# Differential attention with three 128-column products in one PSUM sum, and one reciprocal per attention job

## The chip, the cores and the metric

The kernel runs on one core of one Trainium2 chip. The metric is the device time of one execution in microseconds (us); the median of three runs is used. The core has five engines with an instruction queue each: TensorE (PE, with its weight loads shown apart as PEld), VectorE (DVE), ScalarE (ACT), GpSimd (POOL) and SyncE (SP), which here only issues transfers between the main memory and the on-chip memory. Each queue runs in the order in which it was written; engines wait for each other by semaphores.

## The reference

One layer on x of 1024 tokens by 1024 features: half of a SwiGLU feed-forward block is added, then a mixer, then half of a second feed-forward block, then a norm. The mixer is two attentions side by side. The part that matters:

```
# A: 8 heads of 64, each token sees its chunk of 64 and the 8 chunks before
p = softmax(q k^T / 8 + bias);  o = p v
# B: 4 heads; each has two score sets (q, k of 64) and values v of 128
p = softmax(scores_r + bias)                    # r = 0, 1
attn = p[0] - lam * p[1];  o = attn v
o = rms_norm(o, subln_g) * (1 - lambda_init)
# both
merged = sigmoid(g_A) * (o_A W_A) + sigmoid(g_B) * (o_B W_B)
x = x + merged W_o
```

## The kernel before, in words

All matrix products work on float32 values that are split in two parts, `hi` (rounded) and `lo` (what is left), and a product a·b is formed as hi·hi + hi·lo + lo·hi. The helper `mm3` (L125 to L129) writes these three matmuls into one PSUM sum. The stages follow each other: first feed-forward block, input projection of the mixer, the two attentions, branch and output projections, second feed-forward block, final norm.

The change lies in the attention stage, which runs from about 1121 to 1401 us of the span. Its work is cut in jobs of 128 or 256 query rows. `run` starts a new job at each step and moves up to four live jobs on by one piece each, so scores and softmax of one job stand beside the transposes, value products and norms of older ones. This fixes only the order in which the program is written: the framework then plans each engine's queue with an own model of durations, and so a change in one place reorders all five queues of the stage.

- `jobs_a` makes 32 jobs (8 heads, 4 blocks of 256 rows). A job computes two score tiles `sc`, in `softmax` a minimum on DVE (L692) and the exponential with its row sum `rs` on ACT (L694), then `ri`, the reciprocal of `rs` (L749, DVE), and scales the probabilities `pm` by it on POOL (L750). Two pieces later come the transposes `pt` (L700, PE) with their split in `whi` (ACT) and `wlo` (DVE), and then the value products `pv` (L766).
- `jobs_b` makes 32 jobs (4 heads, 8 blocks of 128 rows; block i sees i + 1 blocks of 128 keys, called kb here, so a head has 36 and the stage 144). It takes two softmaxes, two reciprocals (L824, L826), and forms p[0] + r2·p[1] on DVE (L827, L829), where r2 holds -lam and the ratio of the row sums. After the transposes the values are multiplied. Here `vt` holds the values as 256 columns, first the hi part, then the lo part, and before the change one matmul takes all 256 of them:

```
nc.tensor.matmul(pv, pt[0][:, c], vt[:, kb, :], start=kb == 0, stop=False)                            # L845
nc.tensor.matmul(pv[:, 0:P], pt[1][:, c], vt[:, kb, 0:P], start=False, stop=kb == i)                  # L846
```

  So the left half of `pv` holds hi·hi + lo·hi and the right half hi·lo; two ACT copies (L848, L850) scale them by r1 and POOL adds them (L851). Then follow a sum of squares (L854, DVE), a power and a product on POOL (L138, L857), the transposing product `try` (L860, PE) and the split into `y`.
- `branch_a` is a filler: the output projection of A (`pb`, twelve matmuls of 512 columns each, then a product with the gate `gl` on DVE, L794, and a store `ta`, L795). Every second job of B draws one of its 16 parts.
- The first job of a head loads q, k (hi and lo) and v in `load_qkv` (L123): `qs`, `ks`, `kl`, `vt`, 1 MB each, the first three as two halves. They lie in a pool of 14 buffers of that size, which also holds the results `y` and the bias `nb`. SP issues the loads in its own order, among the loads `gl` and `wa` and the stores `ta`, which wait for DVE.

The pools `rs` and `ri` have four buffers of a few bytes. Before, a job of B takes two of each; the reciprocal r1 is in use until the copies L848 and L850.

Of the kernel before, what the change touches and what calls it, by code (L numbers as in the profile page):

```python
# [53 lines left out]
def hybrid_layer_kernel(ctx, tc, x, ffn1_norm, ffn1_w_in, ffn1_w_out, mix_norm, w_mix_in,  # L54
# [601 lines left out]
    with tc.tile_pool(name="ps2", bufs=1, space=PSUM) as ps:  # L656
# [31 lines left out]
        def softmax(sc, n, nb, dst, rs):  # L688

            mn = small.tile([P, 1], F32, tag="mn", name="mn")  # L690
            d3 = dst.rearrange("p (n w) -> p n w", n=n)
            nc.vector.tensor_tensor_reduce(out=d3, in0=sc, in1=nb.rearrange("p (n w) -> p n w", n=n),  # L692
                                           scale=1.0, scalar=3e38, op0=ALU.add, op1=ALU.min, accum_out=mn)
            nc.scalar.activation(out=dst, in_=dst, func=AF.Exp, bias=mn, scale=-1.0, accum_out=rs)  # L694
# [26 lines left out]
        def jobs_a(pr):  # L721
            ctx_ = {}

            def job(sb_, h):
                if not ctx_:
                    ctx_["qkv"] = load_qkv(pr)
                    ctx_["y"] = big([P, 2, S], "y")
                    ys.append(ctx_["y"])
                    ctx_["nb"] = big([P, 2, S], "nb", F32)
                    for hh in range(2):  # L730
                        bias_rows(ctx_["nb"][:, hh, :WA], diag_a, 2 * pr + hh, EA, WA)
                qkv, y, nb = (ctx_[n] for n in ("qkv", "y", "nb"))
                vt = qkv[3]
                i0, i1 = 2 * sb_, 2 * sb_ + 1
                first = [max(0, i - 4) for i in (i0, i1)]

                slots = [(kb, s) for kb in range(first[1], i0 + 1) for s in range(2)]
                if first[0] < first[1]:
                    slots.append((first[0], 0))
                slots.append((i1, 1))  # L740
                pms = []
                for s, i in enumerate((i0, i1)):
                    w = (i - first[s] + 1) * P
                    sc, n = scores(qkv, h, i, first[s] * P, w)
                    pm = raw_tile([P, D], "pm")[:, :w]
                    rs = small.tile([P, 1], F32, tag="rs", name="rs")
                    softmax(sc, n, nb[:, h, WA - w:WA], pm, rs)
                    ri = small.tile([P, 1], F32, tag="ri", name="ri")
                    nc.vector.reciprocal(out=ri, in_=rs)  # L749
                    nc.gpsimd.tensor_tensor(out=pm, in0=pm, in1=ri.to_broadcast([P, w]), op=ALU.mult)  # L750
                    pms.append(pm)
                yield
                yield
                pts = []
                for u0 in range(0, len(slots), 4):
                    pts.append(transpose_p([pms[s][:, (kb - first[s]) * P:(kb - first[s] + 1) * P]
                                            for kb, s in slots[u0:u0 + 4]]))
                yield
                pv = ps.tile([P, 256], F32, tag="pv", bufs=2, name="pv")
                b = 0  # L760
                while b < len(slots):
                    kb, s = slots[b]
                    nq = 2 if b + 1 < len(slots) and slots[b + 1][0] == kb else 1
                    o = (b % 4) * P
                    for c in range(2):
                        nc.tensor.matmul(pv[:, s * P:(s + nq) * P], vt[:, kb, 128 * h:128 * h + 128],  # L766
                                         pts[b // 4][c][:, o:o + nq * P], start=(b == 0 and c == 0),
                                         stop=(b + nq == len(slots) and c == 1))
                    b += nq

                if h == 0:
                    ctx_["ysum"] = temp([P, 256], "ysum")
                ysum = ctx_["ysum"]
                rh, rl = slice(64 * h, 64 * h + 64), slice(64 - 64 * h, 128 - 64 * h)
                nc.scalar.copy(out=ysum[rh, :], in_=pv[rl, :])
                nc.vector.tensor_tensor(out=ysum[rh, :], in0=pv[rh, :], in1=ysum[rh, :], op=ALU.add)
                if h == 1:
                    c = slice(sb_ * 256, (sb_ + 1) * 256)
                    split(ysum, y[:, 0, c], y[:, 1, c], on_pool=True)
            return [job(sb_, h) for sb_ in range(4) for h in range(2)]  # L780


# [16 lines left out]
        def jobs_b(hb, filler):  # L799
            ctx_ = {}  # L800

            def job(i):
                if not ctx_:
                    ctx_["qkv"] = load_qkv(4 + hb)
                    ctx_["y"] = big([P, 2, S], "y")
                    ys.append(ctx_["y"])
                    if hb % 2 == 0:
                        nbs.append(big([P, 2, S], "nb", F32))
                        for hh in range(2):
                            bias_rows(nbs[-1][:, hh, :], diag_b, hb + hh, EB, WB)  # L810
                    ctx_["nb"] = nbs[-1][:, hb % 2, :]
                qkv, y, nb = (ctx_[n] for n in ("qkv", "y", "nb"))
                vt = qkv[3]
                w = (i + 1) * P
                pr, rs = [], []
                for r in range(2):
                    sc, n = scores(qkv, r, i, 0, w)
                    pm = raw_tile([P, WB], "pm")[:, :w]
                    s_ = small.tile([P, 1], F32, tag="rs", name="rs")
                    softmax(sc, n, nb[:, WB - w:], pm, s_)  # L820
                    pr.append(pm)
                    rs.append(s_)
                r1, r2 = (small.tile([P, 1], F32, tag="ri", name="ri") for _ in range(2))
                nc.vector.reciprocal(out=r1, in_=rs[0])  # L824

                nc.vector.reciprocal(out=r2, in_=rs[1])  # L826
                nc.vector.scalar_tensor_tensor(out=r2, in0=r2, scalar=neg_lam, in1=rs[0],  # L827
                                               op0=ALU.mult, op1=ALU.mult)
                nc.vector.scalar_tensor_tensor(out=pr[0], in0=pr[1], scalar=r2, in1=pr[0],  # L829
                                               op0=ALU.mult, op1=ALU.add)  # L830
                yield
                yield
                pts = []
                for b0 in range(0, i + 1, 4):
                    pts.append(transpose_p([pr[0][:, b * P:(b + 1) * P] for b in range(b0, min(b0 + 4, i + 1))]))
                due[0] += 0.5
                while due[0] >= 1:
                    due[0] -= 1
                    next(filler, None)
                yield  # L840
                pv = ps.tile([P, 256], F32, tag="pv", bufs=2, name="pv")
                for kb in range(i + 1):
                    c = slice((kb % 4) * P, (kb % 4 + 1) * P)
                    pt = pts[kb // 4]
                    nc.tensor.matmul(pv, pt[0][:, c], vt[:, kb, :], start=kb == 0, stop=False)  # L845
                    nc.tensor.matmul(pv[:, 0:P], pt[1][:, c], vt[:, kb, 0:P], start=False, stop=kb == i)  # L846
                o1 = temp([P, P], "o1")
                nc.scalar.activation(out=o1, in_=pv[:, P:], func=AF.Copy, scale=r1)  # L848
                o2 = temp([P, P], "o2")
                nc.scalar.activation(out=o2, in_=pv[:, :P], func=AF.Copy, scale=r1)  # L850
                nc.gpsimd.tensor_tensor(out=o1, in0=o1, in1=o2, op=ALU.add)  # L851
                sq = temp([P, P], "sq")
                v = small.tile([P, 1], F32, tag="v", name="v")
                nc.vector.tensor_tensor_reduce(out=sq, in0=o1, in1=o1, scale=1.0 / P, scalar=EPS,  # L854
                                               op0=ALU.mult, op1=ALU.add, accum_out=v)
                dg = small.tile([P, P], F32, tag="dg", bufs=3, name="dg")
                nc.gpsimd.tensor_tensor(out=dg, in0=ident, in1=rsqrt(v).to_broadcast([P, P]), op=ALU.mult)  # L857
                yield
                tr = ps.tile([P, 4, P], F32, tag="pt", bufs=2, name="try")
                nc.tensor.matmul(tr[:, 0, :], o1, dg, start=True, stop=True)  # L860
                c = slice(i * P, (i + 1) * P)
                split(tr[:, 0, :], y[:, 0, c], y[:, 1, c], scale=gsub)
            return [job(i) for i in range(NT)]
# [115 lines left out]
```

## Time and profile before

| | |
|---|---|
| median of three runs | 2207.89 us (2207.6 to 2208.07) |
| the profiled execution | 2210.82 us, its span 2209.0 us |
| PE, PEld busy | 95%, 81% of the span |
| DVE, ACT, POOL busy | 66%, 45%, 13% |
| granted TensorE clock, mean | 0.979 |
| main memory | 144 GB/s over the span |

The span is the time from the first to the last instruction of the profiled execution. "Busy" adds the times of instructions; matmuls are pipelined, so that a matmul's own time overlaps the next one's, and the distance between the starts of two neighbours says what one of them costs. In a row of the trace, "[5.34 <-DMA ks<-k]" means that the engine stood idle for 5.34 us just before and what ended that. In the tables of waits the columns are the total in us, the number of waits and the longest. In tables of stretches each engine has its busy time and the number of its instructions in brackets, and behind them stand the granted clock, the share of the 16 transfer engines that is busy, and GB/s.

### The profile page before, as it was taken

The page shows a single profiled execution, that of the slowest core. Times are in us where ns is not written, and L with a number is a line of the kernel's source. Part 1 is how long each engine was busy: PE and PEld are TensorE (multiplying, and loading weights), DVE is VectorE, ACT ScalarE, POOL GpSimd, SP SyncE. Part 2 cuts the span into 40 slices and gives each one's busy share as a digit, 9 for nine tenths or more (in the row PEclk, how much of TensorE's full clock was granted, in tenths as well). Part 3 has the DMA queues.
Part 4 walks back from the last instruction along what each step waited for, and adds up shares of the span by engine and source line. Part 5 has one row for each costly group of instructions (what it writes and reads, how often), then busy time and mean ns, then how long its engine had stood idle before and what let it go on. Part 6 is the DMA issues. An engine that isn't in the chain of part 4 may idle for free. (4 is left out here: it accounts for less than half of the span.)

```text
span 2209.0 us, 29778 instructions
## 1 busy us (share of the span) xinstructions
PE 2100.4 (95%) x10373; PEld 1779.8 (81%) x10373; DVE 1448.2 (66%) x2620; ACT 991.2 (45%) x1972; POOL 286.4 (13%) x371
## 2 busy tenths in 40 slices
PE   5999999999997999999999988899799999999997
PEld 4888888888886998888878877788688888888886
DVE  8765656577567756655378877658756565658566
ACT  5433333334445444444478756335433333334444
POOL 6130000000006100000056333104300000000000
PEclk8999999999998999999999989999999999999999
DMA  4374323284353445542497555755423232367335
GB/s 136 100 198 115 119 83 118 96 305 162 115 154 112 134 154 171 172 148 91 120 226 184 125 152 139 225 166 172 119 86 120 88 116 93 111 224 240 97 115 186
DMA packets 262246, 319.72 MB, mean 145 GB/s; under 512 B 16732, under 2 KB 162156, under 8 KB 262096
## 3 DMA queue, kind: packets, MB, share of 16 engines
q1 hardware_dynamic: 257888, 309.91, 45.3%
q0 software_dynamic: 4064, 7.39, 1.5%
q8 instruction: 82, 1.34, 0.3%
q14 instruction: 68, 0.56, 0.1%
q10 hardware_dynamic: 144, 0.52, 0.1%
HBM read 219.44 MB, written 98.30 MB: 144 GB/s over the span
## 5 line engine op out<-in xcount | busy, mean ns | idle before, releaser
L101 DVE TENSOR_TENSOR wlo<-raw,whi 128x512 fp32r<-128x512 f32 x197 | 141.6, 719 | 183.3 <-PE prod L128 109.7
L96 ACT CAST whi<-raw 128x512 fp32r<-128x512 f32 x200 | 124.4, 622 | 273.8 <-PE prod L128 224.5
L96 ACT CAST whi<-T 128x512 fp32r<-128x512 f32 x192 | 119.5, 623 | 282.7 <-PE prod L128 163.0
L128 PE MATMUL po<-wlo,whi 128*128 128x512 f32 x616 | 240.0, 390 | 0.0
L129 PE MATMUL po<-whi,wlo 128*128 128x512 f32 x616 | 239.9, 390 | 0.0
L127 PE MATMUL po<-whi 128*128 128x512 f32 x616 | 236.4, 390 | 0.0
L101 DVE TENSOR_TENSOR wlo<-T,whi 128x512 fp32r<-128x512 f32 x189 | 134.2, 710 | 98.3 <-ACT whi L96 74.4
L112 DVE TENSOR_TENSOR c<-prod,c 128x512 f32<-128x512 f32 (+1 forms) x201 | 133.2, 664 | 99.7 <-PE prod L129 98.7
L101 DVE TENSOR_TENSOR wlo<-B,whi 128x512 fp32r<-128x512 f32 x154 | 107.0, 695 | 129.2 <-ACT whi L96 129.2
L96 ACT CAST whi<-B 128x512 fp32r<-128x512 f32 x154 | 95.7, 622 | 206.9 <-PE po L128 185.3
L138 POOL TENSOR_TENSOR r<-v,neg_half 128x1 f32<-128x1 f32 x64 | 44.3, 693 | 758.9 <-DVE v L155 721.2
L129 PEld LDWEIGHTS po<-whi,wlo 128*128 128x128 f32 x616 | 115.7, 188 | 24.1
L127 PEld LDWEIGHTS po<-whi 128*128 128x128 f32 x616 | 115.7, 188 | 23.9
L128 PEld LDWEIGHTS po<-wlo,whi 128*128 128x128 f32 x616 | 115.7, 188 | 23.8
L184 POOL TENSOR_TENSOR xt<-xt,gain 128x512 f32<-128x512 f32 x36 | 49.1, 1380 | 516.4 <-DMA xt<-xm 484.3
L96 ACT CAST whi<-ha 128x512 fp32r<-128x512 f32 x154 | 94.8, 616 | 39.0 <-PE prod L128 17.2
L101 DVE TENSOR_TENSOR wlo<-ha,whi 128x512 fp32r<-128x512 f32 x154 | 105.7, 687 | 10.0 <-ACT whi L96 10.0
L258 ACT COPY c<-prod 128x512 f32<-128x512 f32 (+1 forms) x201 | 103.3, 573 | 5.2 <-issue 2.6
L694 ACT ACTIVATE pm<-pm,mn 128x640 f32<-128x640 f32 (+7 forms) x128 | 94.1, 736 | 17.4 <-DVE mn L692 16.1
L127 PE MATMUL prod<-S1h,whi 128*128 128x512 f32 (+1 forms) x252 | 96.5, 383 | 2.2 <-ACT S1h L96 2.2
L127 PE MATMUL prod<-S4h,whi 128*128 128x512 f32 (+1 forms) x252 | 96.1, 381 | 1.8 <-ACT c L258 1.8
L127 PE MATMUL prod<-A11h,whi 128*128 128x512 f32 (+1 forms) x252 | 96.8, 384 | 0.7 <-ACT A11h L96 0.7
(247 smaller groups left out, 5835.4 us busy)
## 6 DMA issues: line engine op xcount, KB each, us to landing
raw<-in_ffn_w_in_dram SPq DMA_DIRECT2D x88, 512.0 KB, 3.9
ha<-hS SPq DMA_DIRECT2D x88, 256.0 KB, 2.7
raw<-in_w_mix_in_dram SPq DMA_DIRECT2D x40, 512.0 KB, 4.1
ha<-hA SPq DMA_DIRECT2D x66, 256.0 KB, 2.7
hA<-c SPq DMA_DIRECT2D x64, 256.0 KB, 2.5
B<-in_ffn_w_out_dram SPq DMA_DIRECT2D x12, 1024.0 KB, 5.9
hS<-hs SPq DMA_DIRECT2D x44, 256.0 KB, 2.1
hS<-c SPq DMA_DIRECT2D x42, 256.0 KB, 2.1
```

Of the source, the lines that this page charges most:

```text
L96: nc.scalar.copy(out=hi, in_=src)
L101: (nc.gpsimd if on_pool else nc.vector).tensor_tensor(out=lo, in0=src, in1=h, op=ALU.subtract)
L112: nc.vector.tensor_tensor(out=out_, in0=a, in1=b, op=op)
L127: nc.tensor.matmul(ps, a[0], b[0], start=first, stop=False, skip_group_check=shared)
L128: nc.tensor.matmul(ps, a[0], b[1], start=False, stop=False, skip_group_check=shared)
L129: nc.tensor.matmul(ps, a[1], b[0], start=False, stop=last, skip_group_check=shared)
L138: nc.gpsimd.tensor_tensor(out=r, in0=v, in1=neg_half, op=ALU.pow)
L184: (nc.vector if on_vector else nc.gpsimd).tensor_tensor(out=xt[h][d], in0=xt[h][d], in1=gain[:, c], op=ALU.mult)
L258: nc.scalar.copy(out=self.held[name], in_=p)
L694: nc.scalar.activation(out=dst, in_=dst, func=AF.Exp, bias=mn, scale=-1.0, accum_out=rs)
```

## The change

In B the two matmuls of a kb become the three of `mm3`, each with 128 columns, all into one `pv` of 128 columns; the second ACT copy and the POOL sum go. In both attentions the row sums of a job's two softmaxes lie in one tile `rs` of two columns, and one reciprocal takes both; in A the two POOL products follow it. Since a job now takes one `rs` and one `ri`, the four buffers hold four jobs of B, where they held two.

```
@@ jobs_a
-                pms = []
+                pms, rs = [], small.tile([P, 2], F32, tag="rs", name="rs")
                 for s, i in enumerate((i0, i1)):
...
-                    rs = small.tile([P, 1], F32, tag="rs", name="rs")
-                    softmax(sc, n, nb[:, h, WA - w:WA], pm, rs)
-                    ri = small.tile([P, 1], F32, tag="ri", name="ri")
-                    nc.vector.reciprocal(out=ri, in_=rs)
-                    nc.gpsimd.tensor_tensor(out=pm, in0=pm, in1=ri.to_broadcast([P, w]), op=ALU.mult)
+                    softmax(sc, n, nb[:, h, WA - w:WA], pm, rs[:, s:s + 1])
                     pms.append(pm)
+                ri = small.tile([P, 2], F32, tag="ri", name="ri")
+                nc.vector.reciprocal(out=ri, in_=rs)
+                for s, pm in enumerate(pms):
+                    nc.gpsimd.tensor_tensor(out=pm, in0=pm, in1=ri[:, s:s + 1].to_broadcast(list(pm.shape)),
+                                            op=ALU.mult)
@@ jobs_b
-                r1, r2 = (small.tile([P, 1], F32, tag="ri", name="ri") for _ in range(2))
-                nc.vector.reciprocal(out=r1, in_=rs[0])
-                nc.vector.reciprocal(out=r2, in_=rs[1])
-                nc.vector.scalar_tensor_tensor(out=r2, in0=r2, scalar=neg_lam, in1=rs[0],
+                ri = small.tile([P, 2], F32, tag="ri", name="ri")
+                r1, r2 = ri[:, 0:1], ri[:, 1:2]
+                nc.vector.reciprocal(out=ri, in_=rs)
+                nc.vector.scalar_tensor_tensor(out=r2, in0=r2, scalar=neg_lam, in1=rs[:, 0:1],
                                                op0=ALU.mult, op1=ALU.mult)
@@ jobs_b, value product
-                pv = ps.tile([P, 256], F32, tag="pv", bufs=2, name="pv")
+                pv = ps.tile([P, P], F32, tag="pv", bufs=2, name="pv")
                 for kb in range(i + 1):
                     c = slice((kb % 4) * P, (kb % 4 + 1) * P)
-                    pt = pts[kb // 4]
-                    nc.tensor.matmul(pv, pt[0][:, c], vt[:, kb, :], start=kb == 0, stop=False)
-                    nc.tensor.matmul(pv[:, 0:P], pt[1][:, c], vt[:, kb, 0:P], start=False, stop=kb == i)
+                    mm3(pv, [v[:, c] for v in pts[kb // 4]], (vt[:, kb, 0:P], vt[:, kb, P:]), kb == 0, kb == i)
                 o1 = temp([P, P], "o1")
-                nc.scalar.activation(out=o1, in_=pv[:, P:], func=AF.Copy, scale=r1)
-                o2 = temp([P, P], "o2")
-                nc.scalar.activation(out=o2, in_=pv[:, :P], func=AF.Copy, scale=r1)
-                nc.gpsimd.tensor_tensor(out=o1, in0=o1, in1=o2, op=ALU.add)
+                nc.scalar.activation(out=o1, in_=pv, func=AF.Copy, scale=r1)
```

The planned order moves in the whole attention stage. Three places matter below. The first is TensorE where the second head of B ends and the third begins: the row with `sc` of 128 columns, twice, is the third head's first score. Before:

```order
L845 MATMUL pv<-vt,whi 128x256
L846 MATMUL pv<-vt,wlo 128x128
L700 MATMUL pt<-ident,pm 128x128
L845 MATMUL pv<-vt,whi 128x256
L684 MATMUL sc<-ks,qs 128x128 x2
L860 MATMUL try<-dg,o_12353 128x128
L846 MATMUL pv<-vt,wlo 128x128
L845 MATMUL pv<-vt,whi 128x256
```

and the same place now, where `pv` comes from the lines of `mm3`:

```order
L128 MATMUL pv<-vt,whi 128x128
L129 MATMUL pv<-vt,wlo 128x128
L127 MATMUL pv<-vt,whi 128x128
L128 MATMUL pv<-vt,whi 128x128
L684 MATMUL sc<-ks,qs 128x128 x2
L700 MATMUL pt<-ident,pm 128x128 x4
L129 MATMUL pv<-vt,wlo 128x128
L685 MATMUL sc<-kl,qs 128x128 x2
L700 MATMUL pt<-ident,pm 128x128 x2
```

The `try` and the value products of one older job that stood behind the new head's first score now stand ahead of it, and the second half of that score (L685, which needs `kl`) follows it closely.

The second place is SP's queue where the fourth head of B is loaded (`q_182`, `k_190`). The `ta` rows are the stores that wait for DVE.

```order
+L796 DMA ta_213<-gl 128x512
+L118 DMA wa<-in_w_branch_a_dram 128x4x256
 L118 DMA gl<-g_197 128x512
-L118 DMA wa<-in_w_branch_a_dram 128x4x256
-L795 DMA ta_213<-gl 128x512
 L123 DMA qs<-q_182 64x2x1024
 L123 DMA ks<-k_190 64x2x1024
 L123 DMA qs<-q_182 64x2x1024
 L123 DMA ks<-k_190 64x2x1024
+L796 DMA ta_213<-gl 128x512
+L118 DMA gl<-g_198 128x512
 L123 DMA kl<-k_190 64x2x1024 x2
```

The second store `ta_213` stood ahead of the four loads and now stands behind them.

The third is DVE in the second job pair of A (the `ISA` rows are the minimum of `softmax` and the reading of its result):

```order
 L692 ISA pm,mn<-sc,nb 128x384
 L692 ISA mn 128x1
-L749 RECIPROCAL ri<-rs 128x1
 L692 ISA pm,mn<-sc,nb 128x512
 L692 ISA mn 128x1
-L749 RECIPROCAL ri<-rs 128x1
+L749 RECIPROCAL ri<-rs 128x2
 L101 TENSOR_TENSOR wlo<-pt,whi 128x384
```

One of the two reciprocals is gone, and the one left stands at the place of the later one.

More of the change, by code (lines that the diff above doesn't have):

```diff
@@ L814, in job @@
                 w = (i + 1) * P
-                pr, rs = [], []
+                pr, rs = [], small.tile([P, 2], F32, tag="rs", name="rs")
                 for r in range(2):
@@ L818, in job @@
                     pm = raw_tile([P, WB], "pm")[:, :w]
-                    s_ = small.tile([P, 1], F32, tag="rs", name="rs")
-                    softmax(sc, n, nb[:, WB - w:], pm, s_)
+                    softmax(sc, n, nb[:, WB - w:], pm, rs[:, r:r + 1])
                     pr.append(pm)
-                    rs.append(s_)
-                r1, r2 = (small.tile([P, 1], F32, tag="ri", name="ri") for _ in range(2))
-                nc.vector.reciprocal(out=r1, in_=rs[0])
-                nc.vector.reciprocal(out=r2, in_=rs[1])
-                nc.vector.scalar_tensor_tensor(out=r2, in0=r2, scalar=neg_lam, in1=rs[0],
+                ri = small.tile([P, 2], F32, tag="ri", name="ri")
+                r1, r2 = ri[:, 0:1], ri[:, 1:2]
+                nc.vector.reciprocal(out=ri, in_=rs)
+                nc.vector.scalar_tensor_tensor(out=r2, in0=r2, scalar=neg_lam, in1=rs[:, 0:1],
                                                op0=ALU.mult, op1=ALU.mult)
```

## The prediction

> **What bounds the kernel now.** I read the page first, then the table of stretches over the attention stage, the waits of TensorE there, and the trace row by row where the table shows a hole.
>
> ```profile
> span 2209.0 us, 29778 instructions
> 1121.00:1234.70 113.70, 104.89 (x737) 92.77 (x736) 98.54 (x308) 96.48 (x250) 71.42 (x89) 0.98 0.74 170
> 1234.70:1254.96 20.26, 18.18 (x109) 15.54 (x107) 18.99 (x52) 15.38 (x39) 7.37 (x14) 1.00 1.02 229
> 1254.96:1298.57 43.61, 36.31 (x219) 32.42 (x219) 32.89 (x105) 24.88 (x66) 13.30 (x23) 0.92 0.66 160
> 1298.57:1347.02 48.45, 40.37 (x224) 35.47 (x224) 33.76 (x107) 27.75 (x74) 13.45 (x26) 0.86 0.61 166
> 1347.02:1397.50 50.48, 46.13 (x293) 40.51 (x293) 41.60 (x127) 31.70 (x86) 19.93 (x34) 1.00 0.45 147
> ```
>
> The first stretch is A, the other four are the heads of B, cut where the next head's `kl` lands. In A nothing is full: PE is busy for 104.9 of 113.7 us with overlap counted in, DVE for 98.5, ACT for 96.5. In B, PE leads DVE in all heads but the first (46.1 against 41.6 us in the last), ACT and POOL have much room. The profiled execution took 2210.82 us, 1.82 more than its span and 2.93 more than the median of 2207.89; I carry differences over to the median.
>
> PE in B has two kinds of holes, those of the loads of the next head and small ones:
>
> ```profile
> PE sc L684 <- DMA ks<-k: 11.1, 2, 5.7
> PE pv L845 <- ACT o L850: 3.0, 6, 0.7
> PE sc L685 <- DMA kl<-k: 1.7, 2, 1.2
> PE pv L845 <- DVE ri L824: 1.4, 1, 1.4
> ```
>
> ```profile
> 1254.96 0.44 PE L685 MATMUL sc<-kl,qs 128*128 128x128 f32 x2 [1.17 <-DMA kl<-k]
> ...
> 1294.88 0.69 PE L684 MATMUL sc<-ks,qs 128*128 128x128 f32 x2 [5.34 <-DMA ks<-k]
> 1298.57 0.63 PE L685 MATMUL sc<-kl,qs 128*128 128x128 f32 x2
> ...
> 1342.40 0.66 PE L684 MATMUL sc<-ks,qs 128*128 128x128 f32 x2 [5.72 <-DMA ks<-k]
> 1347.02 0.41 PE L685 MATMUL sc<-kl,qs 128*128 128x128 f32 x2 [0.54 <-DMA kl<-k]
> ```
>
> So B is PE work in a row, stopped at each new head until its loads land. More PE work lengthens B, except for what fits into those stops.
>
> **The change part by part: the value products.** The cost of one matmul is the distance between starts:
>
> ```profile
> 1392.10 0.33 PE L845 MATMUL pv<-vt,whi 128*128 128x256 f32 x1
> 1392.27 0.22 PE L846 MATMUL pv<-vt,wlo 128*128 128x128 f32 x1
> 1392.33 0.34 PE L845 MATMUL pv<-vt,whi 128*128 128x256 f32 x1
> ```
>
> ```profile
> 1233.40 0.28 PE L766 MATMUL pv<-whi,vt 128*128 128x128 f32 x1
> 1233.51 0.27 PE L766 MATMUL pv<-wlo,vt 128*128 128x128 f32 x1
> ```
>
> ```profile
> L845 PEld LDWEIGHTS pv<-vt,whi x144: 186/189/334, 1234.7 to 1397.0; 128*128 128x128 f32 x144
> L846 PEld LDWEIGHTS pv<-vt,wlo x144: 187/192/338, 1234.8 to 1397.1; 128*128 128x128 f32 x144
> ```
>
> A pair L846, L845 takes 0.23 us (1392.10 to 1392.33), with two weight loads: 0.115 us a load. Two products of 128 columns with a load each (1233.40 to 1233.51) take 0.11 too. Halving the columns thus saves nothing; the load sets the pace, and every matmul has its own, as the 144 and 144 loads show. The change makes three loads of the two: 144 more, 144 x 0.115 = 16.6 us more PE work. By the order these fall as 15, 36, 36 and 57 in the four stretches, other PE work staying the same in each: 1.7, 4.1, 4.1 and 6.6 us. The ends of the unknown are nothing, if the third matmul only takes the 0.06 between 1392.27 and 1392.33 and the fuller pipeline hides that, and all 16.6.
>
> The Trainium skill ("TensorE: Matmul & The Clock Gate", Back-to-back issue gap) gives about 81 ns a matmul for a stream of load and matmul pairs with 128 columns. By it three would be 243 ns and the change 144 x 13 ns = 1.9 us, an estimate from that page; the 0.11 us between the rows above speaks against it.
>
> What a stop takes up depends on when the loads start, and SP's queue sets that:
>
> ```profile
> 1245.40 0.62 SPq L123 DMA_DIRECT2D kl<-k  x1
> ...
> 1276.38 0.32 SPq L795 DMA_DIRECT2D ta<-gl  x1
> ...
> 1277.22 0.58 SPq L123 DMA_DIRECT2D qs<-q  x1
> ...
> 1334.12 1.22 SPq L123 DMA_DIRECT2D kl<-k  x2
> ```
>
> First head, +0.6 us. The stop ends with `kl`, issued at 1245.40 and landed at 1254.96. Its issue stays behind the same store, while a transfer of `wa` now goes ahead; 1.7 us of work meet 1.17 us of idle time. Between 0 and 1.7.
>
> Second head, +2.0. The loads of the third head start at 1277.22, when the store of a filler part is through. In the order, DVE's product for that part now stands behind one more score, and PE has 63 value matmuls ahead of that score instead of 42: 21 x 0.115, and four score matmuls at no less than a load each, 0.5, make it 2.9 us later. Against that `wa` now follows the bias instead of preceding `vt`, which frees the transfer engines somewhat; I take 0.9 us for it. PE itself waits 5.34 us here and so takes up its 4.1 us. Between 0 and 4.1.
>
> Third head, +1.0. `qs` and `ks` no longer wait for a second store, so they should be there in time, and `kl` decides: its buffer comes free with the old head's last score, which now has 93 value matmuls ahead of it within the head, not 55, and four more transposes: 42 loads of 0.115 = 4.8 us later. `kl` took 12.9 us from 1334.12 to 1347.02, queued behind `qs` and `ks`; without them the nearest price is the 9.6 us of 1245.40, 3.3 less. That leaves 1.5, less a share of the small waits, 0.5. Between -1.7 (`kl` in half of its 12.9 us) and +4.8.
>
> Last head, +4.0. No load follows, so 6.6 us of work go on the path. Off go waits: `pv` has two buffers, and a new one had to wait for the second copy. The six waits of 3.0 us in all become shorter by the 0.25 us by which the second copy ends after the first (below), half of them here, 0.75; the 1.4 us of L824 goes, since four jobs' reciprocals now have room; 0.4 for better filling. Between +2 and +6.6.
>
> **Copies, sum and reciprocals.**
>
> ```profile
> 1397.46 0.37 ACT L848 ACTIVATE o<-pv,ri 128x128 f32<-128x128 f32 x1 [1.76 <-PE pv L846]
> 1397.72 0.36 ACT L850 ACTIVATE o<-pv,ri 128x128 f32<-128x128 f32 x1
> 1398.16 0.45 POOL L851 TENSOR_TENSOR o<-o,o 128x128 f32<-128x128 f32 x1 [0.50 <-ACT o L850]
> 1398.91 0.28 DVE L854 CUSTOM_DVE_ANT_0 sq<-o 128x128 f32<-128x128 f32 x1
> ```
>
> ```profile
> L850 ACT ACTIVATE o<-pv,ri 128x128 f32<-128x128 f32 x32 | 11.6, 364 | 0.0
> L851 POOL TENSOR_TENSOR o<-o,o 128x128 f32<-128x128 f32 x32 | 15.8, 493 | 78.4 <-ACT o L850 78.4
> L749 DVE RECIPROCAL ri<-rs 128x1 f32<-128x1 f32 x64 | 9.7, 155 | 3.3 <-ACT pm L694 3.0
> ```
>
> The 11.6 us of ACT and 15.8 of POOL lie under PE, which has the longest busy time in three heads of B; they show only in the last job, where nothing covers the chain from copy to norm. There the square starts at 1398.91; without L850 and L851 it starts about 0.3 after the first copy's end at 1397.83, at 1398.1: -0.8 us.
>
> In A, 32 of 64 reciprocals of 0.155 us go: 5.0 us of DVE, which is busy for 87% of A. All 5.0 would come off if DVE alone bounded A, none if the chain through ACT and PE did, and it is near both; I take the middle, -2.5. The first `pm` of a job is now scaled about one softmax later, but the order has two more jobs' scores between reciprocal and transposes, so POOL (71 of 113.7 us) has cover; if that cover were gone, PE would wait in A, at worst about +1. In B 32 reciprocals go, under PE: nothing.
>
> Sum: 0.6 + 2.0 + 1.0 + 4.0 - 0.8 - 2.5 = +4.3 us. From 2210.82 that is 2215.1 for a profiled execution, and 2212.2 against the median, so 2212.
>
> **The rivals.** (1) Nothing is taken up. If the loads of each head start later by as much as PE's work grows, the stops stay as long as they are: +16.6 - 0.8 - 2.5 = +13.3, 2221 us. For it: the stores ahead of the loads wait on filler work that stands behind PE's. Against it: only 2 to 5 us of delay can be counted up to those places.
>
> (2) The stops take up more, and the clock stays up. After the stop in the second head the granted clock is half:
>
> ```profile
> 1296.00:1300.00 4.00, 3.78 (x19) 3.38 (x18) 1.10 (x4) 1.67 (x6) 0.11 (x1) 0.50 1.08 307
> 1300.00:1304.00 4.00, 4.00 (x19) 4.00 (x20) 2.30 (x8) 1.44 (x4) 2.27 (x3) 0.50 1.06 393
> ```
>
> From `kl` at 1298.57 to 1304 it costs 5.4 / 2 = 2.7 us. If the extra work shortens the idle 5.34 us enough, that returns. With A at its best (-5.0), the first two heads at 0, the third at -2.7 and the last at +2: -6.5 with the tail, 2201 us. The point from which it decides is whether PE's idle time at 1289 to 1295 gets short enough to keep the clock; the trace has no stop between 1.2 and 5.3 us that would tell.
>
> The Trainium skill ("TensorE: Matmul & The Clock Gate", What's actually happening) has the clock fall to half after an idle window of about 3.4 us. By that page, 5.34 - 2.1 us of net filling would stay just below it, an estimate.
>
> (3) The third product is nearly free: with the same `whi` as its neighbour it costs no load of its own. Then the heads gain only: -0.8 - 2.5 - 2.2 for the waits, 2202.4 us. Against it: every matmul in the trace has its load, also L127 and L128 of `mm3`, which share theirs. The Trainium skill's 81 ns above belongs here.
>
> **How the numbers follow.** What can be told from no change in this kernel is about 0.2%, 4.4 us. My forecast, chance 0.48, own range 2208 to 2217 by the bounds of its terms taken half each way, lies at the upper edge of that: 0.32 within, 0.16 slower. Rival 1 gets 0.26, slower. Rival 2 gets 0.16: 0.12 faster, 0.04 within. Rival 3 gets 0.10: 0.06 faster, 0.04 within. Together 0.18 faster, 0.40 the same, 0.42 slower. The range 2202 to 2222 reaches from rival 3 to a little past rival 1.
>
> **What would show it.** Right: `pv` in B with 432 matmuls and 432 loads at 0.115 us; the third stop shorter than 5.72 us; the last head longer by about 4; A shorter by about 2.5. Wrong: triples at 0.23 us (rival 3); stops as long as before in all heads and B longer by 16 (rival 1); a clock of 1.00 after the second head's stop (rival 2). It also goes wrong if the new order of A makes PE wait for POOL, or if SP's new order delays a load by more than the few us counted here.

## The result, and the profile after

The changed kernel is slower: 2230.71 us against 2207.98 us (medians of four runs each), a ratio of 1.0096 with a 95% interval of 1.0075 to 1.0117. That is 22.7 us more, where 4 us more were forecast, and above the forecast range. The profiled execution took 2230.97 us, 20.2 more than the profiled one of before.

The table of stretches, cut at the same events as in the prediction (A, then the heads of B at the landing of the next head's `kl`), for the changed kernel; behind the engines' columns stand the granted clock, the share of the transfer engines and GB/s:

```profile
span 2229.2 us, 29929 instructions
1119.50:1233.10 113.60, 105.49 (x742) 92.24 (x741) 97.29 (x278) 97.17 (x252) 71.78 (x89) 1.00 0.75 171
1233.10:1259.00 25.90, 20.16 (x119) 17.39 (x118) 17.61 (x46) 14.16 (x33) 4.53 (x9) 0.93 0.81 189
1259.00:1308.95 49.95, 43.81 (x255) 39.57 (x255) 34.80 (x100) 23.82 (x60) 8.72 (x16) 0.84 0.52 126
1308.95:1358.54 49.59, 42.85 (x258) 39.22 (x259) 33.14 (x98) 25.03 (x65) 9.47 (x18) 0.84 0.67 180
1358.54:1419.40 60.86, 58.28 (x350) 52.20 (x350) 40.10 (x116) 28.64 (x72) 13.01 (x23) 0.87 0.36 115
```

A is as long as before (113.6 against 113.7 us). The heads of B are longer by 5.6, 6.3, 1.1 and 10.4 us. The column of the clock shows what the forecast left out: 0.93, 0.84, 0.84 and 0.87, where before it was 1.00, 0.92, 0.86 and 1.00.

The value products cost what was said. The tile `pv` in the changed kernel (least, median and longest ns of one load, first and last start):

```profile
L127 PEld LDWEIGHTS pv<-vt,whi x144: 186/192/338, 1233.1 to 1419.1; 128*128 128x128 f32 x144
L128 PEld LDWEIGHTS pv<-vt,whi x144: 187/192/333, 1233.2 to 1419.2; 128*128 128x128 f32 x144
L129 PEld LDWEIGHTS pv<-vt,wlo x144: 188/192/338, 1233.3 to 1419.3; 128*128 128x128 f32 x144
```

There are 432 loads, L127 and L128 with the same `whi` among them. TensorE's rows around the three stops of the changed kernel (the places where it waits for a new head's loads) and one small wait near the end show the rest:

```profile
1252.45 0.28 PE L128 MATMUL pv<-vt,whi 128*128 128x128 f32 x1
1255.93 0.69 PE L684 MATMUL sc<-ks,qs 128*128 128x128 f32 x2 [3.19 <-DMA ks<-k]
...
1259.00 0.69 PE L685 MATMUL sc<-kl,qs 128*128 128x128 f32 x2 [0.96 <-DMA kl<-k]
...
1302.86 0.28 PE L128 MATMUL pv<-vt,whi 128*128 128x128 f32 x1
...
1306.53 0.69 PE L684 MATMUL sc<-ks,qs 128*128 128x128 f32 x2 [3.40 <-DMA ks<-k]
...
1351.97 0.45 PE L684 MATMUL sc<-ks,qs 128*128 128x128 f32 x1 [2.52 <-issue]
1355.53 0.47 PE L684 MATMUL sc<-ks,qs 128*128 128x128 f32 x1 [3.11 <-DVE mn L692]
...
1395.80 0.28 PE L128 MATMUL pv<-vt,whi 128*128 128x128 f32 x1
1395.91 0.27 PE L129 MATMUL pv<-vt,wlo 128*128 128x128 f32 x1
...
1398.27 0.33 PE L127 MATMUL pv<-vt,whi 128*128 128x128 f32 x1 [1.28 <-ACT o L845]
...
1399.15 0.41 PE L128 MATMUL pv<-vt,whi 128*128 128x128 f32 x1
1399.36 0.41 PE L129 MATMUL pv<-vt,wlo 128*128 128x128 f32 x1
```

At full clock a value product costs 0.11 us (1395.80 to 1395.91), after the last wait 0.21 (1399.15 to 1399.36). Stretches of the changed kernel at those four places, from the point where the clock has just fallen:

```profile
1255.50:1269.00 13.50, 11.38 (x46) 10.44 (x47) 6.96 (x26) 5.00 (x16) 1.50 (x3) 0.50 0.59 163
...
1303.30:1316.90 13.60, 9.62 (x45) 9.24 (x45) 3.96 (x15) 3.92 (x12) 1.34 (x5) 0.50 1.01 290
...
1351.10:1364.60 13.50, 8.40 (x26) 6.88 (x27) 6.63 (x21) 3.84 (x11) 0.95 (x2) 0.50 0.79 206
...
1398.90:1408.90 10.00, 9.61 (x41) 8.80 (x41) 3.88 (x10) 2.47 (x6) 2.59 (x4) 0.50 0.75 248
```

The second stop became shorter (3.40 us, 5.34 before), the third is as long in two parts (2.52 and 3.11 around one matmul, 5.72 before), and the first, 1.17 us before, grew to 3.19 with 0.96 behind it. With each go 13.5 us or more at half clock, and with the pause of 1.28 us another 10. The clock does not wait for a stop to end: it has fallen by 1255.5, 2.7 us into the first stop, and by 1303.3, when the second had only begun (its last matmul before started at 1302.86 and took 0.28). In the kernel before there were two such stretches in B, shown here by two rows of its table:

```profile
1291.60:1305.10 13.50, 9.94 (x43) 9.14 (x44) 4.64 (x12) 4.17 (x11) 3.53 (x5) 0.50 1.03 290
...
1339.40:1346.00 6.60, 3.60 (x17) 3.63 (x17) 0.42 (x2) 0.37 (x1) 0.00 (x0) 0.50 1.02 211
```

To split the loss, I priced each matmul start of B at its distance to the next at full clock (0.115 us where the load sets the pace, about 0.225 for 512 columns) and called this "work". Work that falls in half-clock time loses as much again, and the rest of the stretch is idle time. This split is worked out, not measured: "work" is a count of matmuls times a price, so it says nothing new about the price, and some matmul records are missing from the traces. From the first to the last value product of B:

| profiled execution | B, us | work | half-clock time | lost to half clock | idle |
|---|---|---|---|---|---|
| before | 162.5 | 126.8 | 20.5 | 7.0 | 28.7 |
| after | 186.3 | 142.8 | 51.2 | 20.4 | 23.1 |

Of the 23.8 us between the two, 16.0 are the third load and 13.4 more are lost to the clock, while 5.6 come back from idle time.

The end of B in the changed kernel shows the shorter chain of the last job, on three engines:

```profile
1419.72 0.37 ACT L845 ACTIVATE o<-pv,ri 128x128 f32<-128x128 f32 x1 [2.09 <-PE pv L129]
...
1420.23 0.29 DVE L848 CUSTOM_DVE_ANT_0 sq<-o 128x128 f32<-128x128 f32 x1 [2.21 <-ACT o L845]
...
1421.69 0.49 PE L854 MATMUL try<-dg,o 128*128 128x128 f32 x2 [1.78 <-POOL dg L851]
```

### The profile page after: what moved, and what is told of

It reads as the page before. It is cut to its first block, busy times and chain, and to the rows that moved or that the text cites. A ratio compares the mean times of both kernels' runs of the same rounds, so it can differ in the third digit from the quotient of the medians.

```text
span 2229.2 us, 29929 instructions
## 1 busy us (share of the span) xinstructions
PE 2120.2 (95%) x10517; PEld 1798.7 (81%) x10517; DVE 1445.7 (65%) x2556; ACT 983.1 (44%) x1940; POOL 267.2 (12%) x339
## 5 line engine op out<-in xcount | busy, mean ns | idle before, releaser
L128 PE MATMUL po<-wlo,whi 128*128 128x512 f32 x616 | 239.6, 389 | 0.0
L127 PE MATMUL po<-whi 128*128 128x512 f32 x616 | 236.1, 389 | 0.0
L128 PEld LDWEIGHTS po<-wlo,whi 128*128 128x128 f32 x616 | 115.6, 188 | 24.2
L127 PEld LDWEIGHTS po<-whi 128*128 128x128 f32 x616 | 115.6, 188 | 24.1
L692 DVE CUSTOM_DVE_ANT_0 pm<-sc,nb 128x640 f32<-128x640 f32 (+7 forms) x128 | 87.9, 701 | 24.8 <-PE sc L685 15.9
L127 PE MATMUL prod<-S1h,whi 128*128 128x512 f32 (+1 forms) x252 | 96.3, 382 | 3.1 <-ACT S1h L96 3.1
L127 PE MATMUL prod<-A11h,whi 128*128 128x512 f32 (+1 forms) x252 | 96.8, 384 | 1.0 <-ACT A11h L96 1.0
```

Source lines behind the costliest of these rows:

```text
L127: nc.tensor.matmul(ps, a[0], b[0], start=first, stop=False, skip_group_check=shared)
L128: nc.tensor.matmul(ps, a[0], b[1], start=False, stop=False, skip_group_check=shared)
```

## Experiments

Every ratio is against the kernel before, run on the same chip. Theory L is the prediction's account with each term near its size; the other names are explained by the expectations.

**One part of the change at a time.** The shared reciprocals alone, with the value products, both copies and the sum as before:

```
-    ri = small.tile([P, 1], ...); nc.vector.reciprocal(out=ri, in_=rs)     # one per softmax
+    ri = small.tile([P, 2], ...); nc.vector.reciprocal(out=ri, in_=rs)     # one per job, A and B
```

> Only the shared reciprocals; the value product of B stays as before (two matmuls of 256 and 128 columns, two copies, sum on POOL). Theory L (the third weight load per key block is what costs): no third load, so within 4 us of before, 2204 to 2212. Theory O (the new order of the queues, which the shared tiles bring, holds back the loads of the next heads): a good part of the 22.7 us stays, 2218 or more.

Measured: 2216.86 us against 2209.62, 1.003 [1.002, 1.004]: 7 us slower, between the two expectations. Less work on DVE made the kernel slower. TensorE has the same matmuls to do in B, and its half-clock time grew from 20.5 to 30.7 us, which by the split costs 6.2 of the 6.9 us by which B is longer. The table of stretches has for nearly all of B, with the clock as the third column from the end (0.94 before):

```profile
1234.00:1404.00 170.00, 145.36 (x841) 128.56 (x841) 126.31 (x360) 99.16 (x260) 53.41 (x97) 0.91 0.59 160
```

The three products alone, with the reciprocals as before:

```
-    nc.tensor.matmul(pv, pt[0][:, c], vt[:, kb, :], ...)                # 256 columns
-    nc.tensor.matmul(pv[:, 0:P], pt[1][:, c], vt[:, kb, 0:P], ...)
+    mm3(pv, [v[:, c] for v in pts[kb // 4]], (vt[:, kb, 0:P], vt[:, kb, P:]), kb == 0, kb == i)
...                                                                      # one copy, no POOL sum
```

> Only the value product: three matmuls of 128 columns in one sum, one copy; reciprocals as before. Theory L: 144 more loads of 0.115 us, 16.6 us, and more half-clock time behind the stops: 2222 to 2234. Theory O: near before, 2205 to 2214.

Measured: 2232.93 us, 1.0102 [1.0087, 1.0117]. The three products alone give the whole loss, and the 7 us of the reciprocals do not add to it.

**The load against the columns.** The changed kernel without the product hi·lo, so two products of 128 columns and two loads for each kb (part of the result is left out):

```
-    mm3(pv, ...)                                                        # three products
+    nc.tensor.matmul(pv, pt[0][:, c], vt[:, kb, 0:P], start=kb == 0, stop=False)
+    nc.tensor.matmul(pv, pt[1][:, c], vt[:, kb, 0:P], start=False, stop=kb == i)
```

> The changed kernel without the product of the hi probabilities with the lo values, which is left out of the result: two matmuls of 128 columns per key block, so two loads as before and a third fewer columns. Theory L: the load sets the pace, so B takes about what it took before, 2202 to 2211 in all. Rival C (columns cost too): 128 columns less at 0.055 us each for 144 key blocks, 8 us faster than before, near 2199. Theory O: the order stays close to that of the changed kernel, 2220 or more.

Measured: 2218.85 us, 1.0041 [1.0027, 1.0056], above the expected time. With the third load gone 12 us come back, but with as many loads as before and fewer columns it is still 9 us slower than before. Of these, 7 are what the shared reciprocals cost alone, if that carries over to this order. Two products still take 0.22 us, where the pair of 256 and 128 columns took 0.23, so fewer columns save next to nothing at full clock:

```profile
1358.79 0.28 PE L845 MATMUL pv<-vt,wlo 128*128 128x128 f32 x1
1358.90 0.27 PE L844 MATMUL pv<-vt,whi 128*128 128x128 f32 x1
1359.01 0.27 PE L845 MATMUL pv<-vt,wlo 128*128 128x128 f32 x1
```

The half-clock time of B is 37.5 us, against 20.5 before and 30.7 with the shared reciprocals alone. B as one stretch of this kernel, with a clock of 0.89:

```profile
1232.20:1402.30 170.10, 144.08 (x836) 126.62 (x835) 125.01 (x359) 91.10 (x229) 35.09 (x66) 0.89 0.58 157
```

The kernel before with its second product issued twice (three loads, and both copies and the sum kept; the doubled term is in the result):

```
     nc.tensor.matmul(pv, pt[0][:, c], vt[:, kb, :], start=kb == 0, stop=False)
+    nc.tensor.matmul(pv[:, 0:P], pt[1][:, c], vt[:, kb, 0:P], start=False, stop=False)
     nc.tensor.matmul(pv[:, 0:P], pt[1][:, c], vt[:, kb, 0:P], start=False, stop=kb == i)
```

> The kernel before with the second matmul of each key block (128 columns) written twice, which adds that product once too often to the result: three loads, all else as before, two copies and the POOL sum included. Theory L: 16.6 us of work and the clock behind it, 2220 to 2234. If instead the changed kernel lost its time through fewer copies and another order: below 2215.

Measured: 2234.66 us, 1.0111 [1.0096, 1.0126]. This is just above the expected range. The third load, with the order that comes with it, costs as much as the whole change. The second copy and the POOL sum can be worth no more than a few us: the three products without them took 2232.93.

**Without the stops.** Both kernels with the q, k and v of B's first head kept for all four heads, so that nothing is loaded inside B (the other heads' results are left out):

```
-    ctx_["qkv"] = load_qkv(4 + hb)
+    if not held:
+        held.append(load_qkv(4))
+    ctx_["qkv"] = held[0]
```

> The kernel before, but all four heads of B use the q, k and v of the first head, so the loads of the three later heads, and with them the stops, are left out (the result of three heads is wrong by that). Theory K (the changed kernel lost 16.6 us by weight loads and the rest by half-clock time behind stops): stops of some 14 us and 3 to 5 us of lost clock go, 2186 to 2195. It is the partner of the next run.

> The changed kernel with the same loads left out. Theory K: without stops the clock stays full and the bare work remains: 12 to 17 us above the run before it, and its trace has no half-clock time in B but at the end. Rival W (the third matmul costs more than a load each, or the new order costs by itself, and the clock only went along): the distance stays 20 us or more.

Measured: 2190.88 us (0.9918 [0.9902, 0.9933]) for the kernel before and 2202.33 us (0.9971 [0.996, 0.9983]) for the changed one. B as one stretch, first the kernel before without loads, then the changed one without loads:

```profile
1231.88:1378.91 147.03, 137.23 (x840) 120.28 (x839) 125.84 (x390) 98.97 (x262) 52.09 (x97) 0.98 0.30 99
```

```profile
1234.33:1393.02 158.69, 152.21 (x980) 136.85 (x979) 123.26 (x359) 90.94 (x229) 37.04 (x66) 0.96 0.28 91
```

The distance between the two kernels falls from 22.7 to 11.4 us, a little below the 12 to 17 expected: without loads, half of the loss is gone, and the clock is 0.98 and 0.96, where with the loads the changed kernel has this row for B:

```profile
1233.10:1419.40 186.30, 165.10 (x981) 148.37 (x979) 125.65 (x359) 91.65 (x229) 35.73 (x66) 0.86 0.55 145
```

By the split, 16.0 us of more work, 4.5 of half clock and 8.8 less idle time (17.9 to 9.1) make the 11.7 us between the two stretches. So the room that I had counted on is there, but in the small waits. Half-clock time does not vanish with the stops, as the expectation had it: 13.7 us of it are left in B of the changed kernel, part of them from 1332 on, in the middle. Leaving the loads out is worth 19 us to the kernel before and 28 to the changed one; with them go their transfers and the old order, not the stops alone.

**Loading earlier.** In both kernels `qs` and `ks` of the next head are loaded with the fifth job of a head instead of with the first job of the next (`kl` and `vt` still at its first job, because of the 14 buffers):

```
+    if i == 4 and hb < 3:
+        load_early(5 + hb)                  # qs, ks
...
-    ctx_["qkv"] = load_qkv(4 + hb)
+    ctx_["qkv"] = load_rest(4 + hb) if hb else load_qkv(4)   # kl, vt
```

> The kernel before with the loads of the next head's qs and ks issued four jobs earlier, when their buffers are free. Theory K: the waits for ks go, those for kl shorten, less half-clock time than the 23.9 us of B before: 2193 to 2204. If the transfers' bandwidth and not their start sets the stops: within 4 us of before.

> The changed kernel with the same earlier loads. Theory K: half-clock time in B falls from 51 to below 35 us, 2207 to 2220. If the clock plays no part beyond the stops: no more gained than the waits for ks are shorter, 2222 to 2227.

Measured: the kernel before with early loads takes 2204.47 us, 0.9977 [0.9967, 0.9986], the changed one 2221.51, 1.006 [1.0041, 1.0079]. The first, 0.5 us above the range expected for it, beats both kernels of this study. The second gains 9 us over the changed kernel, 1.5 us less than the least expected. B as one stretch of the first, and its longest wait for a load:

```profile
1231.69:1388.33 156.64, 140.12 (x840) 122.27 (x839) 126.58 (x390) 98.30 (x262) 53.28 (x96) 0.97 0.57 159
```

```profile
PE sc L707 <- DMA kl<-k: 2.8, 1, 2.8
```

The waits for `ks` (11.1 us before) are gone, and the half-clock time of B is 10.2 instead of 20.5 us (23.9 with the 3.4 us behind the last value product, which the expectation counted in); in the changed kernel it falls from 51.2 to 27.3.

**Is it the columns that keep the clock up?** The changed kernel with all three value products 256 columns wide (the added right half is computed and not used), so with the same 432 loads:

```
-    mm3(pv, ...)
+    for v in range(3):
+        nc.tensor.matmul(pv, pt[v // 2][:, c], vt[:, kb, :], start=kb == 0 and v == 0, stop=kb == i and v == 2)
```

> The changed kernel with all three value matmuls of a key block 256 columns wide (hi probabilities twice, lo once, all over hi and lo values; the result takes the left half and is wrong by that). Loads as in the changed kernel, three per key block, columns double. Theory S (what keeps the clock up is the share of time in which columns stream, not that matmuls are issued): less half-clock time in B than the 51 us of the changed kernel, under 35, and 2214 to 2224 in spite of more columns. Rival: the clock counts matmuls at work, whatever their width: half-clock time 45 us or more, and 2228 to 2236.

Measured: 2225.62 us, 1.0075 [1.006, 1.009]. B as one stretch, and its longest waits for loads:

```profile
1231.42:1411.13 179.71, 157.53 (x980) 142.60 (x979) 124.40 (x359) 92.61 (x229) 36.55 (x66) 0.93 0.56 152
```

```profile
PE sc L684 <- DMA ks<-k: 13.5, 2, 8.1
```

With twice the columns in every value product it is no slower than the changed kernel (5 us less by the medians, though the intervals of the two ratios overlap), although it waits 13.5 us for `ks` where that one waits 6.6. The clock of B is 0.93 instead of 0.86, and the half-clock time 23.9 instead of 51.2 us. So the number of weight loads, 432 in both, does not alone decide how long the clock stays low; that the columns which stream through TensorE do fits. The time lies 1.6 us above what this theory expected, and the planned order differs too, so this run alone leaves it open.

The traces of all 14 kernels here give a second test. In each, every half-clock stretch begins and ends on a regular grid of 3.41 us (the stretches are 3.41, 6.83, 10.24, 13.65 or 17.07 us long in this stage), so a trace can be cut in windows of that length. Between 1100 and 1450 us, 1276 such windows began at full clock. Counted by the columns of the matmuls that start in a window, the clock fell after all 57 with fewer than 2432 columns, after 14 of the 32 with 2432 to 2816, and after none of the 1187 with more. Busy time sorts them less well: of the windows in which TensorE was busy for less than 75%, 71 were followed by a fall and 61 were not. The number of matmuls does not sort them: falls came after as many as 21, and none after some windows with 8. Two windows of the changed kernel, each up to the moment of a fall, show it; TensorE has 19 and 20 matmuls in them and is busy for 2.54 and 2.12 of 3.40 us, but all of them are of 128 columns:

```profile
1299.82:1303.22 3.40, 2.54 (x19) 2.10 (x18) 3.10 (x9) 1.49 (x6) 1.62 (x2) 1.00 1.03 260
1395.40:1398.80 3.40, 2.12 (x20) 1.93 (x18) 3.33 (x8) 2.23 (x5) 0.06 (x1) 1.00 0.12 33
```

From this the margin can be estimated. A window of nothing but 128-column products at 0.115 us holds about 3800 columns, and a pause of about 1 us in it is enough for a fall. With the pairs of 256 and 128 columns in 0.23 us it holds about 5700, and the pause must be nearly 2 us. At half clock a 128-column product takes 0.21 us, which makes some 2080 columns a window, and after none of the 55 half-clock windows with fewer than 2304 columns did the clock come back. So the change also put the value products close to the edge at which the clock falls, and below what brings it back. The count is of windows as the kernels happened to have them; no kernel was built to set the columns of a window alone. Nor do the same edges hold in the other stages: there the clock stayed up after 61 windows with fewer than 2432 columns, all of them made for the larger part of transposing products (`tr`).

**More on top of the early loads.** Three kernels, each built on the kernel before with early loads. With the sum on DVE, which takes the left half of `pv` from PSUM, instead of a second copy and POOL:

```
-    nc.scalar.activation(out=o2, in_=pv[:, :P], func=AF.Copy, scale=r1)
-    nc.gpsimd.tensor_tensor(out=o1, in0=o1, in1=o2, op=ALU.add)
+    nc.vector.scalar_tensor_tensor(out=o1, in0=pv[:, :P], scalar=r1, in1=o2, op0=ALU.mult, op1=ALU.add)
```

> The kernel before with the earlier loads of qs and ks, and the second copy and the POOL sum replaced by one DVE instruction that scales the left half and adds the copied right half. Theory: B is bound by TensorE, so only the waits for the second copy and the tail change: 2199 to 2206, against 2204.5 with the earlier loads alone. If DVE gets too tight in B: 2207 or more.

With the shared reciprocals (the edit shown first):

> The shared reciprocals alone, with the earlier loads of qs and ks. Theory Q (the shared reciprocals cost 7 us only because their order held back the loads): as fast as the earlier loads with separate reciprocals, 2201 to 2208. Rival: the order of the compute queues itself costs, and the 7 us stay: 2210 to 2216.

With the stores `ta` in POOL's queue, so that loads on SP no longer stand behind them:

```
-    nc.sync.dma_start(out=ta_d[j][:, c], in_=gl)
+    nc.gpsimd.dma_start(out=ta_d[j][:, c], in_=gl)
```

> The kernel before with the earlier loads, and the filler's stores issued by POOL, so that kl and vt no longer stand behind them on SP. Theory: kl comes a little earlier, 2198 to 2205. If POOL's issues hold back the norm chain: 2207 or more.

Measured: 2213.7 (1.0017 [1.0008, 1.0027]), 2218.33 (1.0035 [1.0021, 1.0049]) and 2205.42 us (0.9982 [0.9972, 0.9991]). None beats the early loads alone. The sum on DVE costs 9 us, as its second expectation had it, and the shared reciprocals 13, more than either of theirs. For the second of them, the table of TensorE's waits in B shows (us in total, number, longest):

```profile
PE sc L707 <- DMA kl<-k: 9.9, 3, 5.3
PE try L883 <- POOL dg L880: 5.4, 4, 2.2
PE pv L868 <- DVE gl L817: 4.4, 1, 4.4
```

Early loads do not take the cost of the shared reciprocals away: the new order still waits for `kl`, and now for a filler's product on DVE. Why the planner's order is worse with fewer reciprocals stays open.

## Why the prediction failed, point by point

**The step that failed** is what happens to the 16.6 us of third loads. The load term was right: 432 loads at 0.11 us, 16.0 us by the split. What was wrong is that stops and small waits would take up 9.0 of it at no further price. The net of the heads was forecast at 0.6 + 2.0 + 1.0 + 4.0 = 7.6 us; it is 5.6 + 6.3 + 1.1 + 10.4 = 23.4. By the split, idle time gave back 5.6 us, and 13.4 more were lost to the clock, a term that the sum put at nothing. The split follows TensorE and the points below mostly follow the landings; they cut the same time in two ways, so their terms must not be added.

The clock was in the prediction only as a possible gain, in rival 2, with its turning point somewhere between stops of 1.2 and 5.3 us. That the length of a stop decides was the wrong picture: in the changed kernel the clock fell 0.1 us into the second stop, and at the pause of 1.28 us, where few columns had streamed in the 3.41 us before. The profile before had a pause in the gap, too, in A, with the clock at half behind it:

```profile
1189.11 1.09 PE L700 MATMUL pt<-ident,pm 128*128 128x128 f32 x4 [1.59 <-DVE wlo L101]
...
1190.00:1191.70 1.70, 1.70 (x10) 1.70 (x10) 0.70 (x2) 0.59 (x1) 1.61 (x2) 0.50 1.03 200
```

Rival 2 also took the price too low. It read the half clock behind the second stop from 1298.57 to 1304 and got 2.7 us; the stretch lasts from 1291.5 to 1305.1, and by the split B before lost 7.0 us to the clock in both its stretches. In the changed kernel there are three long stretches instead of one long and one short, and one more at the pause of 1.28 us, and more matmuls run in them.

**First head:** forecast +0.6, measured +5.6. `kl` decides its end. It was issued 11.8 us after B's start (1244.87 less 1233.10, in these rows of SP's queue of the changed kernel) against 10.7 before, but it landed at 1259.00, 14.1 us later, against 9.6:

```profile
1238.15 0.38 SPq L118 DMA_DIRECT2D wa<-in_w_branch_a_dram  x1
...
1244.87 0.57 SPq L123 DMA_DIRECT2D kl<-k  x1
...
1289.11 0.58 SPq L123 DMA_DIRECT2D qs<-q  x1
...
1347.40 1.23 SPq L123 DMA_DIRECT2D kl<-k  x2
```

The transfer that takes 4.5 us more is the larger part. By the split, most of this head's loss is more idle time (3.7 us). The `wa` that now goes ahead of the loads, which I had named and priced at nothing, is the likely reason; it was not tried alone.

**Second head:** +2.0 forecast, +6.3 measured. The delay of the next `qs` was counted in part: it was issued 30.1 us after the head's start (1289.11 less 1259.00) against 22.3 before, 7.8 later; 2.9 of that were counted, and the other 5 fit what half clock costs in the 10 us at the head's start. The stop is 1.9 us shorter. Half-clock time in this head is 15.8 us against 7.1.

**Third head:** +1.0 forecast, +1.1 measured. The end is set by `kl`, as named, and most of the 4.2 us of extra work was taken up, but both terms were too large and their errors cancelled, so that the closeness of the number is luck: `kl` was issued 38.5 us after the head's start (1347.40 less 1308.95) instead of 35.6, 2.9 later where 4.8 was counted, and landed within 11.1 us instead of 12.9, 1.8 faster where 3.3 was counted. One wait in this stop was not foreseen. Its second part, 3.11 us, stands behind DVE, which itself waited for the filler's gate `gl`; the new order on SP has that load behind the four of `qs` and `ks`:

```profile
1353.64 0.69 DVE L795 TENSOR_TENSOR gl<-pb,gl 128x512 f32<-128x512 f32 x1 [5.08 <-DMA gl<-g]
```

**Last head:** +4.0 forecast, +10.4 measured: 6.6 of work, as said, and 8.4 lost to the clock by the split, against 4.6 less idle time, where 2.55 had been counted. Before, the clock was 1.00 throughout; now the stretch that began in the third stop and the one from 1398.9 make 16 us of half clock.

**The last job:** -0.8 forecast; from the last value product to the last `try` 3.37 us became 2.54, -0.83.

**A:** -2.5 forecast, measured nothing. 29 reciprocals went, as DVE's group in that stretch of the changed kernel shows (it was 59 of 155 ns before), and A's length did not follow:

```profile
L749 DVE RECIPROCAL ri<-rs 128x2 f32<-128x2 f32 x30 | 4.8, 159 | 2.4 <-ACT pm L694 2.3
```

So DVE's 87% of A did not bound A; my lower bound, none, was the true value, even though A's clock went from 0.98 to 1.00.

**The rivals.** Rival 1 (nothing taken up, 2221 us) was nearest, though not for its reason: 5.6 us were taken up, and 13.4 of clock came on top. Rival 2 had the right object, the clock, with the wrong sign. Rival 3 is excluded by the 432 loads and 0.11 us. The Trainium skill ("TensorE: Matmul & The Clock Gate", What's actually happening) has the clock fall to half after an idle window of about 3.4 us and rise after a busy one of as much. The stretches come in steps of 3.41 us, which agrees with a window of that length. The rest does not fit as it stands: the falls in the changed kernel followed windows that were not idle (TensorE busy for 2.54 of 3.40 us in one), and the way back took 13.65 us three times; the measurement decides. The second stop, put just below the edge in the prediction by an estimate from that page, came out at 3.40 us, but the clock had fallen at its start, before its length could matter.

## What to carry to other kernels

Where each matmul has its own weight load, merging two products in one wide matmul saves loads, and splitting a wide one to save a copy elsewhere costs a load each time; the copy was hidden, the loads were not. Before counting a stop as room for more work, look at the granted clock around it: a stop filled from 5.34 us down to 3.40 was shorter, but still went with 13.65 us at half clock. And look at how many columns the work streams: a run of 128-column products, each with its own load, keeps TensorE busy and still loses the clock at a pause of 1.3 us. A change in any one place of a planned stage should be costed with the new order of the loads, since removing work alone (the reciprocals) cost 7 us here, while earlier loads gained 5 and 9.

## What was not expected of the hardware

The half-clock time was not proportional to the stop: 13.65 us with stops of 3.19, 3.40 and 5.34 us, 6.83 with the one of 5.72, and always a multiple of 3.41. A fall of the clock came with as little as 1.28 us of idle time between value products of 128 columns, at the end of the changed kernel's B; it was seen in the changed kernel without loads too, after a pause of 1.27 us, as a row of TensorE there shows:

```profile
1371.21 0.33 PE L127 MATMUL pv<-vt,whi 128*128 128x128 f32 x1 [1.27 <-ACT o L847]
```

and in its table of stretches, less than 2 us later:

```profile
1373.00:1375.00 2.00, 1.79 (x9) 1.39 (x8) 0.69 (x3) 1.27 (x3) 0.57 (x1) 0.50 1.07 371
```

Matmuls of 256 columns at the same number of loads halved the half-clock time. In the attention stage of all 14 traces the fall of the clock goes with the columns that started in the 3.41 us before it, more closely than with TensorE's busy time or the number of its matmuls. What decides in the narrow range between 2432 and 2816 columns, and how long the way back takes above 2304, stays open: there the clock came back after 71 of 92 windows.
